# Laying the fourth weight block of each gate/up pair 128 bytes off a 256-byte boundary in a one-core hybrid decoder layer

## The chip, the core and the metric

The kernel runs on one core of one Trainium2 chip. The metric is the device time of one execution in microseconds, given as the median of several runs. The profile of one execution comes with a span (first to last instruction) and a time of its own.

## The reference, cut to what matters

One decoder layer on a sequence of 512 positions with 1024 features, in float32: a normalisation, one combined projection, three mixers that run beside each other (a gated MLP over chunks, a sparse attention, a linear recurrence), their gated merge, an output projection with a residual, and then the feed-forward part. The change lies in the last one:

```python
hf = rms_norm(x, g_pre_ffn)
f_gate, f_up = jnp.split(hf @ w_ffn_in, 2, axis=-1)     # 1024 -> 2 x 2816
f = (jax.nn.silu(f_gate) * f_up) @ w_ffn_out            # 2816 -> 1024
return x + rms_norm(f, g_post_ffn)
```

## The kernel before, in words

**Precision.** Every large product is made from two parts: `split(src, hi, lo)` (L124) lets ScalarE (ACT) round the source into `hi` at L125 and VectorE (DVE) put the rest into `lo` at L130. A product is then three matmuls: hi·hi, hi·lo, lo·hi.

**Two operands of a matmul.** Each matmul on TensorE (PE) has a stationary operand, 128 columns of four bytes that a weight load (PEld) puts into the array ahead of it, and a moving operand of 64 to 512 columns that streams through. In this kernel every matmul has a weight load of its own, and the load for the next matmul starts while the present one streams.

**The gate/up pairs.** The 22 column tiles of the gate and of the up projection are taken in pairs. The first two pairs are plain products (`ffn_head`). For the other 20, j from `HEAD` = 2 to 21, the pair's weights and the activations are taken as 2x2 blocks and seven block products are made instead of eight (a Strassen-like scheme). The weight blocks are a11, a12, a21 and a22, each 128 x 512 numbers; `pair_prep(j)` forms their hi and lo parts and those of four sums (`s1` to `s4`). `pairs()` then runs, for each j, the products with a11, s1, a22 of pair j-1 (in `last`), s2, a12, s4 and s3. Each is 12 matmuls with 256 moving columns at L1310 (`product_parts`): four blocks k of the stationary operand, three matmuls each. 20 pairs x 7 products x 12 is 1680 matmuls. The a22 product of the last pair is made after the first matmuls of the down projection.

**Where rows lie.** `row(...)` hands out 128 x 512 four-byte tiles from the pool `mid`, 2048 bytes in each partition: six buffers of the tag `row`, two of `tg`, two of `q32`, in this order. The first `tg` buffer starts at byte 29952, which is 117 x 256. A tag's buffers are used in turn. All other pools but the small constants lie above `mid`. The hi and lo part of a22 are the only stationary operands of the pairs that come from here: hi from `tg`, lo from `q32`. The same two tags hold `mg` gate rows (read by DVE alone), the float32 queries of the compressed attention (`q32`, stationary at L795), and two pairs of sums in the down projection (read by DVE alone). The moving operands of the feed-forward part (`fh`, `fl`, `t`) are laid 64 bytes off a boundary by `MOVED = 16`; most other large operands lie on one.

The residues of the operands' starts modulo 256 bytes, from this layout (steps between a stationary operand's blocks k are 512 bytes, so a residue holds for all of them):

| line | what | stationary | moving | moving columns |
|---|---|---|---|---|
| L1310 | the seven block products, a22 among them | 0 | 64 | 256 |
| L1176 | second half of the plain pairs | 0 | 64 | 256 |
| L773 | attention values | 0 | 0 | 256 |
| L242 | most projections (`passes`) | 0 | 0 | 512 |
| L470 | recurrence gates (`wab`) | 32 | 0 | 512 |
| L882 | transposes in the attention | 0 | 224 | 128 |
| L795 | compressed attention scores (`q32`), float32 | 0 | 0 | 64 |

The order on each engine is the order in which the generators run; `run` and `pairs` interleave them. `prep` of pair j+1 is advanced by `next(prep, None)` between the products of pair j, so a22 of pair j+1 is made during pair j and read during pair j+2.

Of the kernel before, what the change touches and what calls it, by code (L numbers as in the profile page):

```python
# [23 lines left out]
F32 = mybir.dt.float32  # L24
F32R = mybir.dt.float32r
# [5 lines left out]
S = 512  # L31
# [20 lines left out]
def hybrid_block(ctx: ExitStack, tc: tile.TileContext, A, out):  # L52
# [5 lines left out]
    mid = ctx.enter_context(tc.tile_pool(name="mid", bufs=1))  # L58
# [35 lines left out]
    def nm(s):  # L94
        cnt[0] += 1
        return f"{s}_{cnt[0]}"
# [6 lines left out]
        return t if len(shape) == 1 else t.rearrange(  # L103
            "p (a b) -> p a b" if len(shape) == 2 else "p (a b c) -> p a b c", **dict(zip("abc", shape)))

    def row(name, dt=F32, tag="row"):
        return mid.tile([128, S], dt, tag=tag, name=nm(name), bufs={"row": 6, "q32": 2, "tg": 2}[tag])

    def bank(tag):
        return psum[1].tile([128, S], F32, tag=tag, name=nm(tag), bufs=psum[2][tag])  # L110
# [13 lines left out]
    def split(src, hi, lo, lo_eng=None):  # L124
        res["hi"] = SC.activation(hi, src, AF.Copy)  # L125
        e = lo_eng or V
        if e is GP:
            GP.tensor_sub(lo, src, f32(hi))
        else:
            res["lo"] = V.tensor_sub(lo, src, f32(hi))  # L130
# [41 lines left out]
    HEAD, LASTV = 2, 2  # L172
# [186 lines left out]

    rmul = const.tile([128, 3, 4], F32, name="rmul")  # L360
    rbs = row("rbs")
    half = const0([128, 3, 8], "half")

    def norm():

        for i in range(2):
            for c in range(2):
                SC.activation(xr[i][:, c, :], xr[i][:, c, :], AF.Square, accum_out=ssx[:, 2 * i + c:2 * i + c + 1])
            q = slice(2 * i, 2 * i + 2)
            rsqrt(rstd[:, q], ssx[:, q], 2, 1.0 / D, EPS)  # L370
            V.tensor_scalar(rmul[:, 0, q], rstd[:, q], GELU_K ** 0.5, None, op0=OP.mult)
            V.tensor_scalar(rmul[:, 1, q], rstd[:, q], GELU_C, None, op0=OP.mult)
            V.tensor_mul(rmul[:, 2, q], rstd[:, q], rstd[:, q])
            yield
        few = softplus()
        for _ in range(19):
            next(few, None)
            yield
        rb = bank("tr")
        with tc.issue_after(res["mm"].ins):  # L380
            spread(rb, rstd)
        SC.activation(rbs, rb, AF.Copy)
        yield
        for k in range(NK):
            t = row("h32")
            V.scalar_tensor_tensor(t, xt[k], vec[:, V_PRE + k:V_PRE + k + 1], rbs, op0=OP.mult, op1=OP.mult)
            split(t, hh[k], hl[k])
            yield
        V.tensor_scalar(half[:, 0], vec[:, V_BX:V_BX + 8], 0.5, None, op0=OP.mult)
        V.tensor_scalar(half[:, 1], vec[:, V_LNG:V_LNG + 8], 0.5, None, op0=OP.mult)  # L390
        V.tensor_scalar(half[:, 2], vec[:, V_LNB:V_LNB + 8], 0.5, None, op0=OP.mult)
# [31 lines left out]
    def gelu2(x, dst, c=None):  # L423


        s = row("gs")
        SC.activation(s, x, AF.Square, scale=GELU_K ** 0.5 if c is None else rmul[:, 0, c:c + 1])
        V.scalar_tensor_tensor(s, s, 1.0, x, op0=OP.add, op1=OP.mult)
        SC.activation(s, s, AF.Tanh, scale=GELU_C if c is None else rmul[:, 1, c:c + 1])
        V.scalar_tensor_tensor(dst, s, 1.0, x, op0=OP.add, op1=OP.mult)  # L430
# [780 lines left out]
    def first_weights():  # L1211

        ff["raw"] = [slab("rawp", tag="w2", shape=(2, 1024))]
        pair_load(HEAD)
        for _ in range(9):
            yield
        w = [tuple(wts.tile([128, 1024], F32R, tag=t, name=nm(t), bufs=3) for t in ("hi", "lo")) for _ in range(3)]
        ff["ring"] = w
        ff["prep"] = pair_prep(HEAD)
        for _ in range(4):  # L1220
            next(ff["prep"])
            yield
# [45 lines left out]
    def pair_load(j):  # L1268
        if HEAD <= j < NFF:
            SY.dma_start(ff["raw"][(j - HEAD) % 2], A["w_fi"][2 * j:2 * j + 2].rearrange("u p n -> p u n"))  # L1270

    def pair_prep(j):

        if j >= NFF:
            return
        raw = ff["raw"][(j - HEAD) % 2]
        r4 = raw.rearrange("p u (h n) -> p (u h) n", h=2)
        a11, a12, a21, a22 = (r4[:, i] for i in range(4))
        g = [ff["ring"][(3 * (j - HEAD) + i) % 5] for i in range(3)]
        w = wa[j] = {}  # L1280

        def halves(u, *names):
            for i, n in enumerate(names):
                w[n] = tuple(t[:, 512 * i:512 * i + 512] for t in u)

        split(raw[:, 0], *g[0])
        halves(g[0], "a11", "a12")
        s13 = stage.tile([128, 1024], F32, tag="raw", name=nm("s13"), bufs=2)
        V.tensor_tensor(s13.rearrange("p (i n) -> p i n", i=2), r4[:, 0:4:3], a21[:, None, :].to_broadcast([128, 2, 512]),
                        op=OP.subtract)  # L1290
        yield
        split(s13, *g[1])
        halves(g[1], "s3", "s1")
        yield
        w["a22"] = row("a22h", F32R, "tg"), row("a22l", F32R, "q32")
        split(a22, *w["a22"])
        V.tensor_add(a21, s13[:, 512:], a11)
        yield
        V.tensor_sub(a22, a12, a21)
        yield  # L1300
        split(raw[:, 1], *g[2])
        halves(g[2], "s2", "s4")
        pair_load(j + 2)
        yield
# [10 lines left out]
    def pairs():  # L1315
# [11 lines left out]

        for j in range(HEAD, NFF):
            prep = pair_prep(j + 1)
            z, y = ff["zy"] if j == HEAD else (bank("mm")[:, :256], bank("mm"))  # L1330
            r1, r3 = row("r1"), row("r3")
# [405 lines left out]
```

## Time and profile before

| | us |
|---|---|
| median of 3 runs | 1112.24 |
| lowest, highest run | 1109.35, 1112.64 |
| the profiled execution: its own time | 1111.33 |
| the profiled execution: its span | 1109.6 |
| PE busy | 1100.5 (99%) |
| PEld busy | 951.7 (86%) |
| DVE busy | 827.9 (75%) |
| ACT busy | 626.1 (56%) |

Times are read like this. "Busy" joins overlapping instructions of one engine. One matmul lasts longer than the step from its start to the next one's, since they are pipelined; what a run of matmuls costs is therefore the step between starts, called the pitch below, and it is read from the timeline or from the chain of the work that ended last. The granted TensorE clock is 0.998 of full speed over the span.

### The profile page before, as it was taken

The numbers are of one execution on the slowest core, as the hardware profiler recorded it, in microseconds if no ns is written. First come the engines' busy times: TensorE is split into PE (matmuls) and PEld (weight loads), VectorE is DVE, ScalarE is ACT, GpSimd is POOL, SyncE is SP. The second block draws the span as 40 slices with busy tenths as digits, with TensorE's granted clock in tenths as the row PEclk, the third lists the DMA queues.
The fourth block names the chain that finished last, engine by engine and source line by source line (L and its number), as shares of the span: only waits on it lengthen the run. The fifth ranks groups of instructions, "written<-read, shape, count | busy, mean of one in ns | idle before, by whom it ended". The sixth has DMA issues, their size and how long they took to land.

```text
span 1109.6 us, 15969 instructions
## 1 busy us (share of the span) xinstructions
PE 1100.5 (99%) x6152; PEld 951.7 (86%) x6152; DVE 827.9 (75%) x1453; ACT 626.1 (56%) x1120; POOL 46.4 (4%) x59
## 2 busy tenths in 40 slices
PE   9999999999999999999999999999999999999997
PEld 8888778888888887888888888888999999998886
DVE  6966968263575899998998844557988888879665
ACT  6756674232344676876776733435655655567552
POOL 1000203000000000000000000000000000022200
PEclk9999999999999999999999999999999999999999
DMA  8332325323222211102112163331233322378902
GB/s 311 114 95 76 98 94 192 112 82 106 81 91 77 76 58 38 58 20 77 58 39 67 48 241 101 114 115 38 77 115 115 107 104 95 133 192 216 186 33 95
DMA packets 34652, 115.02 MB, mean 104 GB/s; under 512 B 3408, under 2 KB 3696, under 8 KB 33424
## 3 DMA queue, kind: packets, MB, share of 16 engines
q1 hardware_dynamic: 27200, 93.78, 25.4%
q0 software_dynamic: 5216, 11.18, 5.0%
q10 hardware_dynamic: 2160, 9.04, 2.3%
q8 instruction: 48, 0.79, 0.3%
q14 instruction: 28, 0.23, 0.1%
HBM read 111.89 MB, written 2.10 MB: 103 GB/s over the span
## 4 chain that ended last, share of the span: by engine, by line
PE 93%; DVE 4%; ACT 1%; DMA 0%; issue 0%; DVEq 0%
PE mm L242 39%; PE mm L1310 18%; PE mm L1446 7%; PE mm L545 4%; PE mm L1074 4%; PE o L895 4%; PE sc L857 3%; PE tr L882 3%; PE tr L1446 3%; PE mm L773 2%; PE tr L689 1%; PE mm L1176 1%; DVE lo L130 1%; PE tr L470 1%; PE tr L605 1%; PE tr L795 1%
## 5 line engine op out<-in xcount | busy, mean ns | idle before, releaser
L125 ACT ACTIVATE hi<-raw 128x1024 fp32r<-128x1024 f32 (+1 forms) x108 | 113.4, 1050 | 155.4 <-PE mm L242 81.2
L242 PE MATMUL mm<-hh,hi 128*128 128x512 f32 x504 | 199.7, 396 | 0.0
L242 PE MATMUL mm<-hh,lo 128*128 128x512 f32 x504 | 197.5, 392 | 0.2 <-DVE lo L130 0.2
L242 PE MATMUL mm<-hl,hi 128*128 128x512 f32 x504 | 197.1, 391 | 0.0
L130 DVE TENSOR_TENSOR lo<-raw,hi 128x1024 fp32r<-128x1024 f32 (+1 forms) x108 | 132.0, 1222 | 79.3 <-ACT hi L125 72.1
L242 PEld LDWEIGHTS mm<-hh,lo 128*128 128x128 f32 x504 | 94.6, 188 | 19.9 <-DVE lo L130 0.5
L242 PEld LDWEIGHTS mm<-hh,hi 128*128 128x128 f32 x504 | 94.8, 188 | 18.7 <-ACT hi L125 0.4
L242 PEld LDWEIGHTS mm<-hl,hi 128*128 128x128 f32 x504 | 94.7, 188 | 18.4 <-issue 0.2
L863 ACT ACTIVATE P<-P,ast 128x128 f32<-128x128 f32 (+3 forms) x128 | 70.7, 555 | 23.2 <-DVE ast L861 22.6
L861 DVE CUSTOM_DVE_ANT_0 P<-sc,mask 128x128 f32<-128x128 f32 (+3 forms) x128 | 57.9, 484 | 8.2 <-PE sc L857 7.3
L125 ACT ACTIVATE ph<-tr 128x512 fp32r<-128x512 f32 x80 | 47.0, 592 | 29.0 <-PE tr L882 28.1
L130 DVE TENSOR_TENSOR pl<-tr,ph 128x512 fp32r<-128x512 f32 x80 | 54.4, 685 | 4.9 <-ACT ph L125 2.7
L1310 PE MATMUL mm<-t,hi 128*128 128x256 f32 x288 | 52.4, 279 | 0.0
L1397 POOL DMA_DIRECT2D bs<-in_w_fo x16 | 19.3, 1213 | 788.5 <-DVE lo L130 788.5
L857 PE MATMUL sc<-K,q 128*128 128x512 f32 (+2 forms) x192 | 51.0, 368 | 0.0
L1446 PE MATMUL mm<-hi,u 128*128 128x512 f32 x160 | 50.4, 390 | 0.0
L882 PE MATMUL tr<-ident,P 128*128 128x128 f32 x320 | 48.7, 273 | 0.0
L882 PEld LDWEIGHTS tr<-ident,P 128*128 128x128 f32 x320 | 39.1, 140 | 9.7 <-DVE pl L130 1.0
L130 DVE TENSOR_TENSOR lo<-bs,hi 128x1024 fp32r<-128x1024 f32 x28 | 34.1, 1221 | 14.5 <-ACT hi L125 14.5
L1310 PEld LDWEIGHTS mm<-t,hi 128*128 128x128 f32 x288 | 44.0, 188 | 0.0
L1310 PE MATMUL mm<-fh,hi 128*128 128x256 f32 x144 | 40.4, 281 | 0.0
L1310 PE MATMUL mm<-t,lo 128*128 128x256 f32 x144 | 40.3, 280 | 0.0
(384 smaller groups left out, 2752.1 us busy)
## 6 DMA issues: line engine op xcount, KB each, us to landing
raw<-in_w_in SPq DMA_DIRECT2D x64, 512.0 KB, 3.5
rawp<-in_w_fi SPq DMA_DIRECT2D x20, 1024.0 KB, 4.9
raw<-in_w_br SPq DMA_DIRECT2D x24, 512.0 KB, 3.5
bs<-in_w_fo POOLq DMA_DIRECT2D x20, 512.0 KB, 8.0
w<-in_cw ACTq DMA_DIRECT2D x4, 1024.0 KB, 5.1
raw<-in_w_o SPq DMA_DIRECT2D x8, 512.0 KB, 3.5
bs<-in_w_fo SPq DMA_DIRECT2D x8, 512.0 KB, 7.8
raw<-in_w_v SPq DMA_DIRECT2D x7, 512.0 KB, 5.0
```

Of the source, the lines that this page charges most:

```text
L125: res["hi"] = SC.activation(hi, src, AF.Copy)
L130: res["lo"] = V.tensor_sub(lo, src, f32(hi))
L242: res["mm"] = PE.matmul(ps[:m, n0:n1], w[:, k * 128:k * 128 + m], x[k][:, n0:n1], start=(t == 0), stop=(t == 3 * NK - 1))
L545: res["mm"] = PE.matmul(b[c], x[k][:, c * 128:(c + 1) * 128], w[:, kk * 512:kk * 512 + 512], start=(k == 0 and t == 0), stop=(k == NK - 1 ...
L857: PE.matmul(ps[:, :w * n].rearrange("p (b n) -> p b n", b=w), lhs, K[:, i, brs[0]:brs[-1] + 1, :n], start=(i == 0), stop=(i == 1))
L861: V.tensor_tensor_reduce(out=t, in0=ps[:, b * n:b * n + n], in1=mask[0][:, S - n:], scale=-0.125, scalar=3.0e38, op0=OP.add, op1=OP.min, a ...
L863: SC.activation(t, t, AF.Exp, scale=-1.0, bias=st[:, 0, j, b:b + 1], accum_out=st[:, 1, j, b:b + 1])
L882: PE.transpose(pt[:, j * 128:(j + 1) * 128], self.part(j, br)[:, kt * 128:(kt + 1) * 128], ident)
L895: PE.matmul(po, VV[:, kt, g % 2, br].rearrange("p i d -> p (i d)"), x, start=(br == 0 and kt == 0 and t == 0), stop=(br == 1 and kt == a a ...
L1074: res["mm"] = PE.matmul(b[c, f], x[k][:, q], w[:, fs], start=(k == 0 and t == 0), stop=(k == NK - 1 and t == 2))
L1310: res["mm"] = PE.matmul(ps, w[:, k * 128:k * 128 + 128], x[:, k], start=(start and k == t == 0), stop=(k == 3 and t == 2), skip_group_chec ...
L1446: PE.matmul(ps, a, b, start=id(ps) not in begun, stop=i == len(ops) - 1, skip_group_check=True)
```

## The change: two tags get 128 bytes more for each buffer, and a22 takes the half that lies off the boundary

`tg` and `q32` buffers grow from 512 to 544 numbers in each partition (2176 bytes, 8 x 256 + 128). The second buffer of each tag then starts at residue 128, the first at 0. `side` shifts a22's rows by 32 numbers in the first buffer and by none in the second: the `tg` tag has been used 24 times and `q32` 8 times before pair 2, both even, so pair 2 gets the first buffers with `side` = 32, pair 3 the second with 0, and so on. All 20 a22 hi and lo rows start at residue 128.

```diff
-    def row(name, dt=F32, tag="row"):
-        return mid.tile([128, S], dt, tag=tag, name=nm(name), bufs={"row": 6, "q32": 2, "tg": 2}[tag])
+    def row(name, dt=F32, tag="row", first=0):
+        bufs = {"row": 6, "q32": 2, "tg": 2}[tag]
+        return mid.tile([128, S if tag == "row" else S + 32], dt, tag=tag, name=nm(name), bufs=bufs)[:, first:first + S]
...
-        w["a22"] = row("a22h", F32R, "tg"), row("a22l", F32R, "q32")
+        side = 32 * ((j - HEAD + 1) % 2)
+        w["a22"] = row("a22h", F32R, "tg", side), row("a22l", F32R, "q32", side)
```

No instruction is added, removed or moved on any engine or queue, and the waits are the same. Besides a22, two things lie elsewhere: every buffer above the pool `mid` starts 4 x 128 = 512 bytes higher, and the queries in the second `q32` buffer (16 of the 32 float32 matmuls of L795) start at residue 128.

## The prediction

> **What bounds the kernel now.** I read the page's first and fourth part, then the chain of waits cut to the stretch of the pairs, then who waits for whom on PE, and last the timeline of PE at places whose operands lie differently.
>
> The page, busy times and the chain by line:
>
> ```profile
> PE 1100.5 (99%) x6152; PEld 951.7 (86%) x6152; DVE 827.9 (75%) x1453; ACT 626.1 (56%) x1120; POOL 46.4 (4%) x59
> ...
> PE 93%; DVE 4%; ACT 1%; DMA 0%; issue 0%; DVEq 0%
> PE mm L242 39%; PE mm L1310 18%; PE mm L1446 7%; PE mm L545 4%; PE mm L1074 4%; PE o L895 4%; PE sc L857 3%; PE tr L882 3%; PE tr L1446 3%; PE mm L773 2%; PE tr L689 1%; PE mm L1176 1%; DVE lo L130 1%; PE tr L470 1%; PE tr L605 1%; PE tr L795 1%
> ```
>
> PE is the bound, and L1310, the line of the change, is 18% of the chain. The chain in the stretch of the pairs, 797 to 996 us (start, length, what, how many):
>
> ```profile
> 798.03 193.63 PE mm L1310 x1644
> 991.65 2.99 PE mm L1446 x12
> 994.65 1.42 PE mm L1310 x12
> ```
>
> For 193.63 us nothing but L1310's own matmuls stands on the chain. The pitch there is 193.63 us / 1644 = 117.8 ns, and each nanosecond that a matmul of L1310 gains or loses goes into the time in full, as long as nothing comes late to PE. What PE waits for in the whole execution (engine, line waited for, us in total, times, longest):
>
> ```profile
> PE mm L327 <- DVE warm L271: 1.1, 1, 1.1
> PE o L895 <- DVE yb L902: 0.4, 2, 0.2
> PE tr L470 <- ACT ch L125: 0.3, 1, 0.3
> PE mm L242 <- DVE lo L130: 0.2, 1, 0.2
> ```
>
> No wait at L1310 is among them. The a22 rows' own instructions (min/median/max ns, first and last start):
>
> ```profile
> L1310 PEld LDWEIGHTS mm<-t,a22h x160: 187/188/188, 806.2 to 995.6; 128*128 128x128 f32 x160
> L1310 PE MATMUL mm<-t,a22h x160: 279/279/282, 806.3 to 995.7; 128*128 128x256 f32 x160
> L1310 PE MATMUL mm<-t,a22l x80: 279/280/283, 806.6 to 995.8; 128*128 128x256 f32 x80
> L125 ACT ACTIVATE a22h<-rawp x20: 615/632/632, 723.1 to 976.0; 128x512 fp32r<-128x512 f32 x20
> L130 DVE TENSOR_TENSOR a22l<-rawp,a22h x20: 682/689/693, 724.4 to 976.7; 128x512 fp32r<-128x512 f32 x20
> ```
>
> The loads last 188 ns, more than the pitch, so each load lies beside a matmul that still streams: load and matmul both read operands at the same time, all the time. If the place of an operand matters at all, it is there.
>
> **What is changed, in numbers.** 160 + 80 = 240 matmuls of L1310, with their loads, get a stationary operand at residue 128 beside a moving one at 64. The other 1440 stay at 0 and 64. Of the 240 loads, one in twelve runs beside the matmul before the product, and the first load after the product is an old one beside an a22 matmul; 240 overlaps of a load with a matmul are touched. The first term of the sum is 240 times the change of pitch, and the trace has no matmul with a stationary operand at 128. So I bound it by the rows with other residues.
>
> The same residues as the pairs, 0 and 64, in other tiles (PE's timeline in the plain pairs):
>
> ```profile
> 787.09 0.40 PE L1176 MATMUL mm<-fh,u 128*128 128x256 f32 x2
> ...
> 787.80 0.40 PE L1176 MATMUL mm<-fh,u 128*128 128x256 f32 x2
> ```
>
> Six steps in 0.71 us, 118 ns: as in the pairs. Both operands at 0, with 256 columns (the attention values, the first and the last of 13 starts):
>
> ```profile
> 350.25 0.28 PE L773 MATMUL mm<-lo,hh 128*128 128x256 f32 x1
> ...
> 351.69 0.28 PE L773 MATMUL mm<-lo,hh 128*128 128x256 f32 x1
> ```
>
> 12 steps in 1.44 us: 120.0 ns. Against 117.8 this is the only pair of rows with the same shape and other residues, and it differs by 2.2 ns. Both at 0 with 512 columns, and a stationary operand at 32 with 512 columns:
>
> ```profile
> 100.72 0.39 PE L242 MATMUL mm<-hh,hi 128*128 128x512 f32 x1
> ...
> 102.53 0.39 PE L242 MATMUL mm<-hh,lo 128*128 128x512 f32 x1
> ```
>
> ```profile
> 81.47 0.39 PE L470 MATMUL tr<-ch,wabh 128*128 128x512 f32 x1
> 81.70 0.39 PE L470 MATMUL tr<-cl,wabh 128*128 128x512 f32 x1
> ...
> 82.86 0.39 PE L632 MATMUL mm<-hh,hi 128*128 128x512 f32 x1
> ```
>
> 8 steps in 1.81 us, 226 ns, against 6 steps in 1.39 us, 232 ns. A stationary operand that starts 32 bytes off the boundary costs about 5.4 ns a matmul there, if the residue is the reason. Last, what a pitch cannot go under while each matmul has a load of 128 columns (transposes, eight in one row; one lasts 273 ns by the page's groups):
>
> ```profile
> 381.44 1.03 PE L882 MATMUL tr<-ident,P 128*128 128x128 f32 x8
> L882 PE MATMUL tr<-ident,P 128*128 128x128 f32 x320 | 48.7, 273 | 0.0
> ```
>
> The eight cover 1.03 us, so the pitch is (1.03 - 0.27) / 7 = 109 ns, with half the moving columns of L1310. It is the load that sets this.
>
> **The sum.** Term 1, the a22 matmuls. Lower end: the pitch falls to the 109 ns of the loads, 240 x (109 - 117.8) ns = -2.1 us. Upper end: it rises by the 5.4 ns of L470, 240 x 5.4 ns = +1.3 us. The nearest row is L773: same shape, same engine state, and there a shift of 64 bytes between the two operands' starts was worth 2.2 ns, either way 240 x 2.2 ns = 0.5 us. Which way is not to be had from the rows: before, the moving operand starts 64 bytes after the stationary one's residue, and now 64 bytes before it. The distance is the same and only its sign changes, so I take 0 and keep +-0.5 us as the likeliest case's own range.
>
> The Trainium skill ("TensorE: Matmul & The Clock Gate", "Step-by-step: what each phase is for") says that TensorE has two independent read ports into the on-chip memory, one for the moving operand and one for the weight load, and that loading the next weights takes no bandwidth from the running matmul. By this rule no residue could matter, and the term would be 0 exactly. The trace agrees only roughly: 118 against 120 ns at one shape is small but is not nothing. The value of 0 above was taken from the rows, and by the rule the sum would be the same, without the bounds.
>
> Term 2, the writes into a22. ACT's 20 of 632 ns and DVE's 20 of 689 ns now write to residue 128. The last is written by 977 us and read from 994 us on, and in the pairs it is ACT that waits for PE and not the other way round. Even twice as long, 0.69 us more in a pair of 84 matmuls (9.9 us), would have to fill DVE's idle time first:
>
> ```profile
> 846.00:896.00 50.00, 50.00 (x427) 50.00 (x426) 42.30 (x53) 30.08 (x53) 0.00 (x0) 1.00 0.34 120
> ```
>
> In these 50 us (PE, PEld, DVE, ACT, POOL busy) DVE has 7.7 us to spare, 1.5 us a pair, and ACT more. Cost: 0. If that cover were gone, PE would get a22 late, but that is read more than a whole pair later.
>
> Term 3, the 16 float32 matmuls of L795, two passes each, with `q32` at residue 128: 32 passes, by the same 5.4 ns upwards at most 0.2 us, and by the 8.8 ns of the lower end at most 0.3 us downwards. Taken as 0.
>
> Term 4, all pools above `mid` 512 bytes higher. Residues modulo 256 stay as they are, and so do distances between operands in these pools. The blocks k of a22 alternate between two places 512 bytes apart before the change too, and min, median and max of their matmuls (279/279/282) show no such difference. Transfers land 512 bytes higher; PE waits for none of them by the list above, which holds 2.0 us in all. Taken as 0.
>
> Sum: 0 + 0 + 0 + 0, against the profiled execution's 1111.33 us (span 1109.6 and 1.7 us around it). The median of the three runs is 0.9 us higher, 1112.24, so I forecast 1112.2 us.
>
> **The rivals.**
>
> Rival 1, the clash of load and stream goes away for a22. For it: 117.8 is 8.8 ns over the loads' pitch, so something costs, and the place of operands moved it by 2.2 ns once. Against: a shift of 64 bytes regained only a fifth of it, and the 1440 others are left. All of it gives 1112.2 - 2.1 = 1110.1 us, with L773's step once more 1111.7. Neither is 0.3% (3.3 us).
>
> Rival 2, a22 gets the dearer meeting of the two, as L470 suggests. For it: L470's 232 ns at 32 bytes. Against: L470 has 512 columns and mixes with other work, and 128 keeps rows on the same 64-byte steps as 0, which 32 does not. It gives 1112.2 + 1.3 = 1113.5 us.
>
> Rival 3, slower than can be overlooked: at residue 128 the load loses its cover, so that it no longer runs beside the stream. Load alone 109 ns (L882), 256 columns alone about 226 - 120 = 106 ns (L242 less L773, the price of 256 more columns), so one after the other 215 ns, 97 ns more: 240 x 97 ns = 23 us, 1135.5 us. It decides from 3.3 us / 240 = 14 ns a matmul on, a pitch of 132 ns. Against: the worst residue seen costs 5.4 ns, and L470's loads at 32 are hidden as well as all others.
>
> Rival 4, faster by more than 0.3%: what is moved by 512 bytes (term 4) meets less than before in many places. 6152 matmuls would need 0.5 ns each on average. Nothing in the rows speaks for it; against it, blocks 512 bytes apart already show the same durations. It would give 1108.5 us or less.
>
> **How the numbers follow.** Likeliest case, pitch of a22 within 2.2 ns: 0.60. Rival 1: 0.16. Rival 2, widened up to 14 ns: 0.16. Rival 3: 0.04. Rival 4: 0.04. A measurement of this kernel can tell about 0.3%, 3.3 us, from no change: the three runs alone lie 3.3 us apart. Faster by more is rival 4, 0.04; slower by more is rival 3, 0.04; the rest is 0.92, of which I move 0.01 to each side for the runs' own spread: 0.05, 0.90, 0.05. The range: the likeliest case alone is 1111.7 to 1112.7. Rival 1's full price takes the lower end to 1110.1, and the runs' spread below their median (1112.24 - 1109.35 = 2.9 us) could carry a median of three a further 1.1 down, to 1109.0. Above, rival 2 gives 1113.5 and the spread another 1.0: 1114.5.
>
> **What would show it.** In the profile after, the first and the last row of an a22 product in the timeline (12 matmuls before: 845.92 to 847.33 us in the fence below) should again be 1.41 us apart, and the chain's L1310 row should again come to 117.8 ns.
>
> ```profile
> 845.92 0.40 PE L1310 MATMUL mm<-t,a22h 128*128 128x256 f32 x2
> ...
> 847.33 0.40 PE L1310 MATMUL mm<-t,hi 128*128 128x256 f32 x2
> ```
>
> 1.31 us would be rival 1, 1.48 us rival 2, over 1.58 us rival 3; other rows of L1310, L242 or L895 with a new pitch would be rival 4. A wait of PE at L1310 for ACT or DVE would show term 2 wrong. The prediction is wrong by much only if a stationary operand at 128 behaves unlike any residue in this trace.

## The result and the profile after

| | before | after |
|---|---|---|
| median | 1112.44 us of 4 runs (1109.35 to 1112.67) | 1104.51 us of 4 runs (1104.02 to 1106.86) |
| ratio after / before | | 0.9939, 95% interval 0.9917 to 0.9962 |
| profiled execution: time, span | 1111.33, 1109.6 us | 1104.02, 1102.3 us |

The change made the kernel 0.6% faster, and the forecast (1112.2 us, range 1109.0 to 1114.5) missed it. The page after, its busy times and chain (lines after L106 and L1296 are one and two higher than before, so L1312 is the old L1310):

```profile
PE 1093.0 (99%) x6152; PEld 944.4 (86%) x6152; DVE 828.4 (75%) x1453; ACT 624.9 (57%) x1120; POOL 46.5 (4%) x59
...
PE 96%; DVE 2%; ACT 1%; issue 0%; DVEq 0%; ACTq 0%
PE mm L243 42%; PE mm L1312 17%; PE mm L1448 7%; PE mm L546 4%; PE mm L1075 4%; PE o L896 4%; PE sc L858 3%; PE tr L883 3%; PE tr L1448 3%; PE mm L774 2%; PE tr L690 1%; PE mm L1177 1%; PE tr L471 1%; PE tr L606 1%; PE tr L796 1%; DVE lo L131 1%
```

PE is busy 7.5 us less with the same 6152 matmuls, and the span is 7.3 us shorter. The chain in the stretch of the pairs shows where:

```profile
786.95 10.58 PE mm L1177 x92
797.53 182.55 PE mm L1312 x1607
```

The pitch of L1312 is 182.55 us / 1607 = 113.6 ns, where it was 117.8. That is 4.2 ns less on each of the 1680 matmuls of the pairs, 7.0 us, and not on the 240 of a22 alone. Each product has it, not just a22's, as the groups of L1312 between 835 and 982 us show (min/median/max ns; before it was 279 or 280 for all):

```profile
L1312 PE MATMUL mm<-t,u x228: 276/276/276, 835.9 to 979.9; 128*128 128x256 f32 x114
L1312 PE MATMUL mm<-t,a22h x126: 276/276/276, 834.8 to 978.4; 128*128 128x256 f32 x126
L1312 PE MATMUL mm<-fh,hi x112: 276/276/276, 837.2 to 981.0; 128*128 128x256 f32 x112
```

The most useful view was the count of matmuls in a stretch in which PE never rests. Two or three of a count reach over an edge of the stretch, so the pitch is about its length over the count less 2. The columns are the stretch, its length, busy us and count of PE, PEld, DVE, ACT and POOL, the granted clock, the DMA share and GB/s. After:

```profile
788.00:822.00 34.00, 34.00 (x302) 34.00 (x301) 31.46 (x38) 19.93 (x32) 0.00 (x0) 1.00 0.18 63
826.00:834.00 8.00, 8.00 (x70) 8.00 (x69) 7.78 (x10) 5.54 (x9) 0.00 (x0) 1.00 0.40 141
836.00:980.00 144.00, 144.00 (x1273) 144.00 (x1272) 122.53 (x153) 86.81 (x151) 2.48 (x2) 1.00 0.32 115
```

113.3, 117.6 and 113.3 ns: the old pitch is there too, for one pair. Before, a single one held all the time, 190 us / 1614 = 117.7 ns, at the same granted clock of 1.00:

```profile
800.00:990.00 190.00, 190.00 (x1616) 190.00 (x1615) 155.31 (x193) 112.22 (x193) 2.48 (x2) 1.00 0.33 113
```

The sign that the prediction named, 1.41 us from the first row of an a22 product to the first row behind it, came out at 1.36 us, 12 steps of 113.3 ns:

```profile
844.03 0.39 PE L1312 MATMUL mm<-t,a22h 128*128 128x256 f32 x2
...
845.39 0.39 PE L1312 MATMUL mm<-t,hi 128*128 128x256 f32 x2
```

So TensorE runs the same matmuls at one of two pitches, 117.8 or 113.3 ns, and can stay with one for a thousand matmuls. The three changes of pitch in the trace after, in PE's timeline, are these. At 789 us, in the plain pairs, ahead of every a22 product:

```profile
789.03 0.40 PE L1177 MATMUL mm<-fh,u 128*128 128x256 f32 x2
789.26 0.34 PE L1177 MATMUL mm<-fl,u 128*128 128x256 f32 x1
789.44 0.39 PE L1177 MATMUL mm<-fh,u 128*128 128x256 f32 x2
789.67 0.28 PE L1177 MATMUL mm<-fl,u 128*128 128x256 f32 x1
```

From 789.26 it takes 0.18 us to the next start, a delay of about 0.06 us, and the first stretch above shows the lower pitch behind it. The trace of before has the same delay at the same matmul (0.18 us from 789.44) and keeps its pitch, so the delay alone does not decide. Back to 117.8 ns at 824.6 us, where the first a22h row comes late (two matmuls in 0.28 us, 824.57 to 824.85); and to 113.3 ns again at 834.50 us, at the first matmul of the next a22 product, with no stall:

```profile
824.57 0.44 PE L1312 MATMUL mm<-t,a22h 128*128 128x256 f32 x2
824.85 0.28 PE L1312 MATMUL mm<-t,a22l 128*128 128x256 f32 x1
...
834.50 0.39 PE L1312 MATMUL mm<-t,a22h 128*128 128x256 f32 x2
834.73 0.28 PE L1312 MATMUL mm<-t,a22l 128*128 128x256 f32 x1
```

### The profile page after: what moved, and what is told of

The parts are those of the page before. It is cut to its first block, busy times and chain, and to the rows that moved or that the text cites. A ratio compares the mean times of both kernels' runs of the same rounds, so it can differ in the third digit from the quotient of the medians.

```text
span 1102.3 us, 15969 instructions
## 1 busy us (share of the span) xinstructions
PE 1093.0 (99%) x6152; PEld 944.4 (86%) x6152; DVE 828.4 (75%) x1453; ACT 624.9 (57%) x1120; POOL 46.5 (4%) x59
## 4 chain that ended last, share of the span: by engine, by line
PE 96%; DVE 2%; ACT 1%; issue 0%; DVEq 0%; ACTq 0%
PE mm L243 42%; PE mm L1312 17%; PE mm L1448 7%; PE mm L546 4%; PE mm L1075 4%; PE o L896 4%; PE sc L858 3%; PE tr L883 3%; PE tr L1448 3%; PE mm L774 2%; PE tr L690 1%; PE mm L1177 1%; PE tr L471 1%; PE tr L606 1%; PE tr L796 1%; DVE lo L131 1%
## 5 line engine op out<-in xcount | busy, mean ns | idle before, releaser
L1312 PE MATMUL mm<-t,hi 128*128 128x256 f32 x288 | 50.8, 276 | 0.0
L1312 PEld LDWEIGHTS mm<-t,hi 128*128 128x128 f32 x288 | 43.3, 188 | 0.0
L1312 PE MATMUL mm<-fh,hi 128*128 128x256 f32 x144 | 40.1, 278 | 0.0
L1312 PE MATMUL mm<-fh,lo 128*128 128x256 f32 x144 | 39.8, 276 | 0.0
```

What stands on the lines that cost most here:

```text
L1312: res["mm"] = PE.matmul(ps, w[:, k * 128:k * 128 + 128], x[:, k], start=(start and k == t == 0), stop=(k == 3 and t == 2), skip_group_chec ...
```

## The experiments

Three theories were set against each other, named in the expectations. S: a step of the stationary operand's residue moves PE to the lower pitch. M: the 512-byte move of all pools does. C: chance at the stall near 789 us (the delay just shown). From the fifth run on S is sharpened to R: a step only gives a chance, the lower pitch keeps itself until PE has to wait, and the next step renews the chance.

**e1, all of the change but its point.**

```diff
-        side = 32 * ((j - HEAD + 1) % 2)
+        side = 32 * ((j - HEAD) % 2)
```

> All of the change but its point: the wider buffers and the 512-byte shift stay, the a22 rows are all at residue 0 (side = 32*((j-HEAD)%2)). Theory S (step): TensorE has two pitches for the 256-column matmuls of the feed-forward part, 117.8 ns and 113.3 ns, each keeps itself, and a step of the stationary operand's residue moves PE from the first to the second. Then without steps PE stays at 117.8 ns in the pairs: about 1112 us. Theory M (move): the 512-byte shift of all pools above makes the lower pitch possible, a22 has no part: about 1104.5 us, 113.3 ns from about 788 us on. Theory C (chance): a stall of PE before the pairs puts it at either pitch by chance: anything between, runs that differ by up to 8 us.

1111.41 us, ratio 0.9997 (0.9979 to 1.0014). The row of the pairs is that of before, 190 us / 1614:

```profile
800.00:990.00 190.00, 190.00 (x1616) 190.00 (x1615) 155.35 (x193) 112.21 (x193) 2.48 (x2) 1.00 0.34 114
```

M falls: wider buffers and moved pools do nothing that this run can tell. But one of the 11 runs took 1103.54 us, and so did one of the 29 runs of the kernel before in these comparisons, 1103.30. The lower pitch can be had without any step, now and then. That part of C is true.

**e2, a22 at 128 for pair 2 alone.**

```diff
-        side = 32 * ((j - HEAD + 1) % 2)
+        side = 32 * ((j - HEAD + (j == HEAD)) % 2)
```

> a22 at residue 128 for pair 2 alone, at 0 for the other 19 pairs, all else as in the change. Theory S with a pitch that keeps itself: after pair 2's a22 product (about 806 us) the pitch is 113.3 ns and stays, unless a stall of PE throws it back; about 1104.5 to 1107 us. Theory S with a pitch that has to be renewed in each pair: back at 117.8 ns within a pair or at the first stall, 1110 to 1112 us. Theory M: 1104.5 us with the lower pitch from before pair 2's product on. Theory C: anything between.

1110.33 us (1109.78 to 1111.34), ratio 0.9992 (0.9984 to 1.0001). In the trace the pitch stays at 117.7 ns right through pair 2's product and to the end (x1616 between 800 and 990 us, as above). So a step does not always do it, and one step early on was worth little: 1.2 us by the medians, with an interval that takes in no change. S in the plain form falls. Four of the 11 runs were under 1110.0 us, against two of the 29 of before, so the step may have taken in some of the runs that were not traced.

**e3, a short matmul in each a22 product, all residues as before.**

```diff
-                res["mm"] = PE.matmul(ps, w[:, k * 128:k * 128 + 128], x[:, k], start=(start and k == t == 0),
+                cuts = ((0, 128), (128, 256)) if a == "a22" and k == t == 0 else ((0, 256),)
+                for c0, c1 in cuts:
+                    res["mm"] = PE.matmul(ps[:, c0:c1], w[:, k * 128:k * 128 + 128], x[:, k, c0:c1], ...
```

> The kernel before, all at residue 0 and nothing shifted; the first matmul of each a22 product is cut into two of 128 columns, so one short matmul with its load stands in each pair (20 more, about 20 x 105 ns = 2.1 us at most). Theory S in its wider form (anything that shifts the phase between load and stream can move PE to the other pitch): a change of pitch at one of the first cuts, 1106 to 1108 us. Theory S in its narrow form (only the residue does it): 117.8 ns throughout, 1113 to 1114.5 us. Theory M: 1113 to 1114.5 us as well.

1113.0 us median; the 12 runs fall into two heaps, four from 1106.77 to 1107.43 and eight from 1112.47 to 1113.73. The profiled one is of the second: 20 breaks of the rhythm, and at none of them did the pitch change. Where the first four got the lower pitch was not seen. Only two of the 29 runs of before were under 1110 us, so a break may give PE a chance as well; no run here settles it. The gap between the heaps, 6 us, is about what the upper pitch costs over most of the pairs.

**e4, the change once more.**

> The changed kernel once more, for a second trace and more times. Theory S: 113.3 ns from the first or second a22 product on, and back to it in the next a22 product after each throw-back; 1104 to 1107 us. Theory C: the place where the pitch changes has nothing to do with the a22 products, and some executions are as slow as before, 1112 us. Theory M: the lower pitch from before the first a22 product, as in the first trace (788 us).

1105.19 us (1103.83 to 1106.15), ratio 0.9942 (0.9930 to 0.9954). None of the nine runs of the change is above 1106.9 us. The trace has 113.3 ns from 789 us on as in the first one, and this time nothing that PE waits for loses it for longer than a product. The longest wait, in the list of PE's waits and in the timeline (a22h's product, the wait in brackets), and then the stretch behind it:

```profile
PE mm L1312 <- ACT r L1370: 0.7, 1, 0.7
```

```profile
940.16 0.50 PE L1312 MATMUL mm<-t,a22h 128*128 128x256 f32 x2 [0.72 <-ACT r L1370]
```

```profile
941.00:957.00 16.00, 16.00 (x144) 16.00 (x143) 13.65 (x18) 8.39 (x17) 0.00 (x0) 1.00 0.34 128
```

Right behind it, 16 us / 142 = 113 ns. The wait is for ACT's copy at L1370 out of the accumulator to which the a22 product goes on adding. At the lower pitch some a22 products start late; in the trace of before none does.

**e5, a22 at 128 for pair 12 alone.**

```diff
-        side = 32 * ((j - HEAD + 1) % 2)
+        side = 32 * ((j - HEAD + (j == 12)) % 2)
```

> a22 at residue 128 for pair 12 alone, whose a22 product starts at about 905 us; all else as in the kernel with a22 at 0 and the same wider buffers. Theory R (a step of residue gives PE a chance to move to 113.3 ns, the pitch then keeps itself until PE has to wait for its feeders, which happens in the first few pairs alone): 117.8 ns up to about 905 us and 113.3 ns from there to the end of the pairs, 720 x 4.45 ns = 3.2 us less, about 1108 us. Theory C (the pitch is set by chance at PE's stall at 788 us, a22 has no part): nothing happens at 905 us, most runs 1110.5 to 1112 us.

1110.94 us (1108.88 to 1112.16), ratio 0.9989 (0.9981 to 0.9998). Three stretches of the trace:

```profile
875.00:903.00 28.00, 28.00 (x240) 28.00 (x239) 22.28 (x29) 15.45 (x27) 0.00 (x0) 1.00 0.30 102
908.00:941.00 33.00, 33.00 (x294) 33.00 (x293) 27.55 (x35) 18.53 (x32) 0.00 (x0) 1.00 0.29 97
945.00:988.00 43.00, 43.00 (x368) 43.00 (x367) 33.85 (x44) 25.74 (x45) 2.48 (x2) 1.00 0.44 147
```

117.6, then 113.0, then 117.5 ns. The first change stands exactly at pair 12's a22 product, where the expectation put it; twelve u rows of the old pitch end there, and behind the first three matmuls the new one begins (two steps of a22h in 0.24 us, then in 0.23):

```profile
903.49 1.57 PE L1312 MATMUL mm<-t,u 128*128 128x256 f32 x12
904.90 0.40 PE L1312 MATMUL mm<-t,a22h 128*128 128x256 f32 x2
905.14 0.28 PE L1312 MATMUL mm<-t,a22l 128*128 128x256 f32 x1
905.26 0.39 PE L1312 MATMUL mm<-t,a22h 128*128 128x256 f32 x2
905.49 0.28 PE L1312 MATMUL mm<-t,a22l 128*128 128x256 f32 x1
```

The second change is a late a22 product of a later pair, which lies at 0 and so brings no new chance:

```profile
943.00 0.49 PE L1312 MATMUL mm<-t,a22h 128*128 128x256 f32 x2
943.33 0.28 PE L1312 MATMUL mm<-t,a22l 128*128 128x256 f32 x1
```

Two steps in 0.33 us, and the pitch is 117.5 ns from there to the end. The expectation had such late starts in the first few pairs alone; this one is in pair 16. Four of the 11 runs were under 1110.0 us, against one of the 29 of before beside them, so by the times the step took in something like a third of the executions (an estimate from these counts).

**e6, a22's hi rows at 128, its lo rows at 0.**

```diff
-        w["a22"] = row("a22h", F32R, "tg", side), row("a22l", F32R, "q32", side)
+        w["a22"] = row("a22h", F32R, "tg", side), row("a22l", F32R, "q32", 32 - side)
```

> a22's hi rows at residue 128, its lo rows at 0, for all pairs; so the stationary operand steps eight times within each a22 product. Theory R: at least as many chances as with the change, about 1104 to 1106 us. A theory by which both rows must lie at 128 (the place itself and not the step): slower than the change, 1108 to 1112 us. Theory C: 1110.5 to 1112 us.

1105.31 us (1104.87 to 1106.50), ratio 0.9943 (0.9931 to 0.9956), as good as the change. The pitch is upper until pair 2's a22 product at 806 us and lower from there on, in the trace with 15 us / 128 = 117 ns before it and 35 us / 310 = 113 ns behind:

```profile
790.00:805.00 15.00, 15.00 (x130) 15.00 (x129) 15.00 (x17) 9.68 (x14) 0.00 (x0) 1.00 0.00 1
808.00:843.00 35.00, 35.00 (x312) 35.00 (x311) 28.56 (x37) 19.82 (x35) 0.00 (x0) 1.00 0.33 120
```

**e7, a22's hi rows at 64, where the moving operand starts too.** Here `tg` buffers are 64 numbers wider and `q32` ones as before, which moves the pools by the same 512 bytes.

```diff
-        return mid.tile([128, S if tag == "row" else S + 32], ...
+        return mid.tile([128, S + 64 if tag == "tg" else S], ...
-        w["a22"] = row("a22h", F32R, "tg", side), row("a22l", F32R, "q32", side)
+        w["a22"] = row("a22h", F32R, "tg", 16), row("a22l", F32R, "q32")
```

> a22's hi rows at residue 64, where the moving operand starts as well, its lo rows at 0, for all pairs; pools above are 512 bytes higher as in the change. Theory R with any step: about 1104 to 1106 us. Theory R with a step that must end at 128: as before, 1110.5 to 1112 us. Theory C: 1110.5 to 1112 us.

1111.11 us (1107.91 to 1113.16), ratio 0.9992 (0.9984 to 1.0001). A step to 64 does not do it. The trace shows more: this execution had got the lower pitch at 789 us by itself, lost it at a late a22 product at 815.6 us, and none of the 17 later a22 products up to 990 us brought it back:

```profile
790.00:804.00 14.00, 14.00 (x126) 14.00 (x126) 14.00 (x17) 8.94 (x12) 0.00 (x0) 1.00 0.00 1
...
816.00:990.00 174.00, 174.00 (x1479) 174.00 (x1478) 141.79 (x177) 101.83 (x177) 2.48 (x2) 1.00 0.35 118
```

The kernel before may do the same in part of its executions: a microsecond gained by chance and then lost for good. While the lower pitch held, the a22h matmuls with both starts at 64 took 120 ns each (0.24 us for two), and the lo one between them, at 0, still 0.11:

```profile
806.04 0.40 PE L1312 MATMUL mm<-t,a22h 128*128 128x256 f32 x2
806.28 0.28 PE L1312 MATMUL mm<-t,a22l 128*128 128x256 f32 x1
806.39 0.40 PE L1312 MATMUL mm<-t,a22h 128*128 128x256 f32 x2
```

**e8 to e11, other starts of the moving operand.** Each changes `MOVED` (in numbers of four bytes) and nothing else, e9 on top of the change, the others on the kernel before.

```diff
-    MOVED = 16
+    MOVED = 48        # e8 and e9; 32 in e10, 0 in e11
```

> The kernel before with the moving operands of the feed-forward part at residue 192 and not at 64 (MOVED = 48), all stationary ones at 0. If the two pitches belong to the meeting of load and stream at the distance 64: another upper pitch than 117.8 ns, between 113.3 and 120 ns, from 769 us on, and 1104 to 1115 us. If the distance has no part: 117.8 ns and 1111.5 us.

> The change with the moving operands of the feed-forward part at 192 and not at 64 (MOVED = 48): a22 at 128, the other stationary operands at 0. Theory R (a step of the a22 rows to 128 lets PE move from 117.8 to 113.3 ns, and renews it after each throw-back): as the change, 113.3 ns soon after the first a22 product at the latest, 1103.5 to 1106 us, with few or no runs at 1110 us as the kernel with MOVED = 48 alone had. A theory by which it is the distance between a22's start and the moving operand's (192 in the change, 64 here) that renews: runs at 1109 to 1112 us remain.

> The kernel before with the moving operands of the feed-forward part at residue 128 (MOVED = 32), all stationary ones at 0. If a distance of 128 leaves only the lower pitch: 113.3 ns from 769 us on, 1103 to 1104 us in every run. If it has the two pitches that 64 and 192 have: runs at 1103 to 1104 us and at 1110 to 1112 us. If only distances of 64 and 192 are good: up to 120 ns and 1115 us.

> The kernel before with the moving operands of the feed-forward part at residue 0, as all stationary ones (MOVED = 0). If equal starts give one pitch of 120 ns (as in the attention values, and as in the a22 products of the kernel with a22's hi rows at 64): 120 ns from 769 us on, no 113.3 ns anywhere, 1776 x 2.2 ns = 3.9 us more than before, 1115.5 us, and runs within about 1.5 us of each other. If the two pitches have nothing to do with the places: 117.8 or 113.3 ns, 1104 to 1112 us.

| run | moving, a22, other stationary | us, median (range) | ratio, interval | pitch in its trace |
|---|---|---|---|---|
| before | 64, 0, 0 | 1111.4 to 1111.75 | | 117.8 |
| e8 | 192, 0, 0 | 1109.67 (1103.40 to 1111.77) | 0.9968 (0.9949 to 0.9987) | 113.3, from 789 us on 117.8 |
| e9 | 192, 128, 0 | 1104.07 (1103.42 to 1106.09) | 0.9937 (0.9923 to 0.9950) | 113.3 nearly throughout |
| e10 | 128, 0, 0 | 1114.90 (1112.75 to 1116.13) | 1.0027 (1.0018 to 1.0036) | 118.7, from 789 us on 120.0 |
| e11 | 0, 0, 0 | 1115.16 (1114.60 to 1116.64) | 1.0033 (1.0021 to 1.0045) | 120.0 |

(The times of before are its medians in these comparisons.) One row of the pairs for e11 (e10 has the same count), two for e8, and two starts of e10 ahead of the pairs:

```profile
800.00:990.00 190.00, 190.00 (x1585) 190.00 (x1585) 153.91 (x191) 109.92 (x189) 2.48 (x2) 1.00 0.32 109
```

```profile
771.00:779.00 8.00, 8.00 (x73) 8.00 (x72) 7.77 (x18) 5.87 (x18) 0.00 (x0) 1.00 0.00 0
...
900.00:940.00 40.00, 40.00 (x342) 40.00 (x341) 32.88 (x42) 23.22 (x40) 0.00 (x0) 1.00 0.31 106
```

```profile
770.98 0.29 PE L242 MATMUL mm<-fl,u 128*128 128x256 f32 x1
...
780.95 0.28 PE L242 MATMUL mm<-fl,u 128*128 128x256 f32 x1
```

190 us / 1583 = 120.0 ns in e11: equal starts give one pitch, ahead of the pairs and in them (e11's expectation stated 3.9 us more than before, and 3.8 were measured). Starts that differ by 128 bytes have 120.0 ns in the pairs too, but not only that: ahead of the pairs e10 makes 84 steps in 9.97 us, 118.7 ns, and goes over to 120.0 ns at the stall near 789 us. Three of its 11 runs took 1112.75 to 1113.38 us, which would fit a stay at 118.7 ns; none of them was traced. In e8, 8 us / 71 = 113 ns ahead of the pairs and 40 us / 340 = 117.6 ns in them: 64 and 192 give the two pitches. e8's runs lie in two heaps, five from 1103.40 to 1104.39 and seven from 1109.65 to 1111.77. With a22 at 128 (e9) no run is left in the upper heap, though e9 has only five runs and ran on another chip than e8 (before took 1111.4 us beside the one and 1111.61 beside the other). So the distance of a22 from the moving operand, 192 in the change and 64 in e9, is not what renews; a22's step from 0 to 128 is common to both. e8's five lowest runs are as short as e9's with no step at all, so in them the lower pitch must have lasted through nearly all of the pairs; none was traced. e9's median is the lowest here, but it is not told apart from the change's 1104.51 and 1105.19.

**e12, a22 at 128 for the pairs 12 to 21.**

```diff
-        side = 32 * ((j - HEAD + 1) % 2)
+        side = 32 * ((j - HEAD + (j >= 12)) % 2)
```

> a22 at residue 128 for the pairs 12 to 21, at 0 for the pairs 2 to 11. Theory R with a chance at each step that is well under 1 (e2 and e5 had one step each, and only part of their runs gained): 117.8 ns up to about 905 us, then 113.3 ns from pair 12's a22 product or one of the next two on, and back to it after a throw-back; nearly every run 1108 to 1109.5 us, where e5's lay between 1108.9 and 1112.2 us. If e5's change of pitch at 905 us was chance: as before, 1110.5 to 1112 us in most runs.

1108.65 us (1107.62 to 1109.46), ratio 0.9972 (0.9962 to 0.9983), while the 12 runs of before beside it lay from 1109.85 to 1112.49. The trace:

```profile
790.00:813.00 23.00, 23.00 (x205) 23.00 (x204) 21.29 (x25) 13.85 (x21) 0.00 (x0) 1.00 0.14 47
816.00:904.00 88.00, 88.00 (x748) 88.00 (x748) 73.36 (x91) 51.06 (x90) 0.00 (x0) 1.00 0.31 108
915.00:985.00 70.00, 70.00 (x620) 70.00 (x619) 58.48 (x75) 41.75 (x73) 2.48 (x2) 1.00 0.38 128
```

113, 118 and 113 ns. By chance it began low, lost it at a late a22 product at 816 us, and stayed at the upper pitch over eight more a22 products at 0. Pair 12's step, at about 905 us, did not take; pair 13's, at 915 us, did. This is R with its chance under 1, and it shows the renewal by itself.

**All a22 products together.** In the traces with the moving operands at 64 or 192 (e3 with its cuts left out), PE came to an a22 product of the pairs 2 to 20 at the upper pitch 120 times. With a22's hi rows at 0 or at 64 the pitch behind the product was the upper one in all 114 cases. With them at 128 it was the lower one in four of six (after, e5, e6 and e12; not in e2 and not at pair 12 of e12). And of the ten products that PE reached at the lower pitch but started late, the seven with hi rows at 128 (in after, e4, e6 and e9) were followed by the lower pitch in six cases, the three with rows at 0 or 64 (e5, e7 and e12) in none. So the step to 128 inside the a22 product is what brings the lower pitch back.

## Why the prediction was wrong

**The step that failed is the count on which term 1 rests**: "240 overlaps of a load with a matmul are touched", while the other 1440 "stay at 0 and 64" and so were taken to keep their pitch. They did stay there, and their pitch fell all the same. The prediction took the pitch of a matmul for a property of its own operands. That held only for equal starts (120.0 ns throughout e11). At 64 and 192 PE has two pitches for the same operands, and which one holds depends on what went before. The a22 products, a seventh of the pairs, renew the lower one for the other six sevenths. Term 1 was put at 0, between -2.1 and +1.3 us; the runs showed 4.2 ns less on each of the 1680 matmuls, 7.0 us, which no sum over 240 matmuls within these bounds reaches.

**The bounds were read from the wrong rows.** The lower end of 109 ns came from the transposes. The pitch that was reached is 113.3 ns, close to half of L242's 226 ns for 512 columns; whether that is more than a coincidence no run shows. I took L242 less L773 (106 ns) as the price of 256 columns, with L773's 120 ns, the dear meeting of equal starts, in it. L773 was the right neighbour for e10 and e11, which cost 3.5 and 3.8 us, and was not between the change's two values at all. L470's 5.4 ns at residue 32 had no part in anything that was run. That a moving operand 64 bytes after the stationary one and one 64 bytes before it are the same meeting did hold as far as the two pitches go: e8 has them both.

**A clue was explained away.** The three runs shown lay 3.3 us apart, and I called this the spread of the measurement. A lower pitch by chance can make such differences: in the comparisons three runs of before took 1103.3, 1106.6 and 1108.4 us. In the trace of before all 1644 matmuls stand at 117.8 ns, which looks like a constant. What a trace of one execution shows is one draw.

**The rivals.** Rival 1 had the sign (the clash goes away) and the wrong reach, a22 alone, so it stopped at 2.1 us. Rival 4, faster by more than 0.3% (that is 1108.9 us or less, and not 1108.5), had the right size, was given 0.04, and named the wrong mechanism: with the same 512 bytes e1 took what before took. Rivals 2 and 3 did not happen. The sign that was named for rival 4, other rows of L1310 with a new pitch, is what the trace after showed.

**What held.** PE is the bound, and each nanosecond of the pairs' pitch went into the time: 7.5 us less PE busy, 7.3 us less span. The writes into a22 cost nothing (ACT's 632 ns stayed 632, DVE's 689 became 688). Terms 3 and 4 were 0 as far as e1, which has both, can tell them: 1111.41 us against 1111.53. The lower pitch brought a cost that the prediction had only as a sentence: at 113.3 ns some a22 products start late (PE waited 0.7 us for ACT once in e4), and each late start can throw the pitch back.

The Trainium skill ("TensorE: Matmul & The Clock Gate", "Step-by-step: what each phase is for") says that loading the next weights takes no read bandwidth from the running matmul. The prediction drew from it that no residue could matter, and in these traces one does: the same shape runs at 120.0, 117.8 or 113.3 ns, by where the two operands start and by what went before, and the measurement decides. Whether it is read bandwidth that a matmul at a higher pitch loses, no run shows.

**What stays open.** Why two pitches are stable at distances 64 and 192, why a step from 0 to 128 can lead from the upper to the lower one and none to 64 was seen to, and what decides at the stall near 789 us: four of the ten traces with the moving operands at 64 changed there and six didn't, whatever a22's place. In both traces of the change it was this stall, and not an a22 product, that brought the lower pitch first; the a22 products kept it. No run here shows what happens inside the engine.

## What to carry to other kernels

Where a weight load runs beside every matmul of this shape, try the two operands' starts 64 or 192 bytes apart modulo 256 (113.3 or 117.8 ns here) before the same residue (120.0 ns) or 128 apart (118.7 or 120.0 ns); other distances were not run with this shape. If the runs scatter by several microseconds at the same granted clock, look for a second pitch: count matmuls in stretches without idle time, and run the kernel often. A small irregularity that comes round again can be worth more than a better average place, as it was here: it gave the engine a new chance after each late start.

## What the hardware showed that had not been expected

- Two stable pitches of the same 128 x 256 matmul with a load each, 117.8 and 113.3 ns, at the same granted clock; the longest stretch seen at the lower one is over 1300 matmuls, at the upper one over 1700.
- One pitch of 120.0 ns where both operands start at the same residue of 256 bytes (0 and 0 in e11; 64 and 64 in e7's a22h rows while the lower pitch held), and 118.7 or 120.0 ns where they start 128 apart (e10).
- A delay of a matmul's start by about 0.05 us went with a change of pitch, upwards at 824.6 us and downwards at 789 us in the trace after. The same delay near 789 us changed nothing in six of ten traces, and neither did a break by a shorter matmul (e3, 20 of them) in the trace taken.
